# Inverse roots of the norms: a power on GpSimd in place of an integer guess and Newton steps on VectorE

## The chip, the cores and the metric

The kernel runs on one core of one Trainium2 chip. The metric is the device time of one execution in microseconds (us), as the median of several runs. Engine names are those of the profile: PE is TensorE (matmuls), PEld its weight loads, DVE is VectorE, ACT is ScalarE, POOL is GpSimd, SP is SyncE, which issues most of the DMAs.

## The reference

One inference step of a decoder layer with two groups of heads side by side: 2048 prompt rows of width 1024, and 8 single-row samples with states of their own. Cut to what matters here:

```python
EPS = 1e-6
def _rmsnorm(x, g):
    y = x * rsqrt(mean(x * x, axis=-1) + EPS)
    return y * g

hn = _rmsnorm(x, g_norm) * (1 + scale) + shift       # norm over 1024 columns
z = hn @ w_in                                        # one combined input projection
xa, za, q, k, v, glr, zg = split(z)
...                                                  # group 1: convolution, gates, linear recurrence
o, S_new = gla_chunked(q, k, v, log_alpha, S0)       # group 2: gated linear attention, 4 heads
o = o * rsqrt(mean(o * o, axis=-1) + EPS) * g_gla    # norm over a head's 256 columns
y_gla = o * silu(zg)
mix = concat([y_lru, y_gla]) @ w_out
x = x + gate * mix
return _rmsnorm(x, g_final), the new states
```

So there are three norms. The change touches the first (over x, 1024 columns) and the second (over each head's `o`, 256 columns). The final norm is computed by a function of its own, which is not changed.

## The kernel before

The 2048 rows are worked on in two halves of 1024. Rows lie on the 128 partitions wherever a norm is taken, so a sum of squares is one number per row and per tile, and an inverse root acts on a tile of 128 rows and one to four columns. The program has five stages in time: the start (the first half of x is loaded, normalized, transposed on PE and modulated, while PE computes the modulation from `w_ada`), half 0 (projections, then attention head by head in the order 3, 0, 1, 2, and the recurrence, in between the matmuls of the projections), half 1 (the same, with the samples), and from about 1119 us the output projection with residual and final norm, which is dense PE work.

`rsqrt` (L144) turns sums of squares `ss` into inverse roots `out`. It is called 37 times: five times at the start (`normalize` and `scales`, for pairs of 128-row tiles, `rs<-ss` 128x2, and once for the samples, 8x1), eight times in `turn_ahead` (L269: the second half of x, one tile of 128 rows at a time, while the first is worked on; `rs<-ss` 128x1), twenty times in `gla_norm` (L1138: for one head and one segment of rows, `ors<-oss`, 128x4 in half 0, 128x3 and 128x2 in half 1) and four times in `sample_out` (128x1). The sums of squares come from ACT (`junk` L173, an activation that accumulates).

Who waits for the result:
- At the start `times` (L187, its operation L189) multiplies x by it, and PE's transposes `tp<-ident,x` (L222) wait for that.
- In `turn_ahead` the products are transposed on DVE (L289) and stored; when the tile's buffer `xt` is free, SP loads the next one (L272), and ACT takes its squares (L173) in the midst of its other work.
- In `gla_norm` the attention output `on` is multiplied by it (L1143), and PE transposes `on` (L1217) after that.

Attention runs over segments of 512 rows in half 0, and of 384, 384 and 264 rows in half 1 (the last with the samples). `gla_start` (L1085) makes a segment's masked scores `am` (L1099), their rounded part `amh` (ACT) and the rest `aml` (L1102), and the transposed keys with rounded part `kTh` (ACT) and rest `kTl` (L1105). `gla_chunk` (L1111) then gives PE six or seven matmuls for 128 rows, in this order: `pkv` with `kTh` (L1121, L1122) and with `kTl` (L1123), then `po` with the state `S`, `amh` and `aml` (L1126 to L1129). DVE updates `S` (L1131, L1132) and copies `po` to `on` (L1135). The norm of a segment stands in time beside the `gla_start` of the next.

The order of instructions is set in three ways. Every engine runs its instructions strictly in order. The start is written in blocks marked `in_order`, which keep the written order on each engine. After it, work beside the projections is put on a clock (`after`, `tick`) and handed to a scheduler at build time, which orders the instructions of each engine by its own estimates of durations. So a change of one function may move instructions of others. POOL's queue also issues DMAs: weight loads and stores (`tr` L826, `twd` L838, `wd` L918, `r` L883), gate rows (`zs` L1265, `zgd` L1208), states. What stands behind a DMA issue that waits, waits too.

## Time and profile before

| | |
|---|---|
| median of 3 runs | 1440.75 us (1440.42 to 1440.96) |
| span of the profiled execution | 1444.3 us |
| PE busy | 1415.9 us, 98% |
| DVE busy | 1081.8 us, 75%, 2551 instructions |
| ACT busy | 678.9 us, 47% |
| POOL busy | 220.9 us, 15%, 362 instructions |
| PE's granted clock | 9 tenths or more in all 40 slices |

Of the profiled execution the page gives the span, and no separate time. All times of day below ("at 850 us") are from the start of that span. A row of the timeline reads: start, duration, engine, line, operation, output and inputs by the program's names, shape, count, and in brackets how long the engine sat idle before it and what it waited for last. A row may group several instructions of one kind, and the duration is then from the first's start to the last's end. The table of waits gives for each pair of waiting instruction and releaser the sum, the number of times and the longest.

### The profile page before, as it was taken

How to read it: one execution, taken by the hardware profiler on the slowest of the kernel's cores; microseconds unless marked ns; L12 is line 12 of the kernel's file. 1: busy time of each engine (PE TensorE's matmuls, PEld its weight loads, DVE VectorE, ACT ScalarE, POOL GpSimd, SP SyncE). 2: the span in 40 equal slices, each digit the busy share in tenths (PEclk: the TensorE clock that was granted, in tenths of full speed). 3: DMA queues.
4: the chain of work that ended last, by engine and by line, in shares of the span. 5: the costliest groups of instructions: out<-in, count | busy, mean ns of one | idle time of the engine just before them, and what ended most of it. 6: DMA issues, size and time to landing. Idle time of an engine off the chain costs nothing.

```text
span 1444.3 us, 23546 instructions
## 1 busy us (share of the span) xinstructions
PE 1415.9 (98%) x8677; PEld 1246.5 (86%) x8677; DVE 1081.8 (75%) x2551; ACT 678.9 (47%) x1227; POOL 220.9 (15%) x362
## 2 busy tenths in 40 slices
PE   7999999999999999999999999999999999999998
PEld 5889979888888988788899999999998887788886
DVE  5767658987798778935458688686888986688886
ACT  3653454653365255524354454635566622154342
POOL 0200112221112114000111422333210000000000
PEclk9999999999999999999999999999999999999999
DMA  9755785885676568567744665665671767694452
GB/s 328 271 186 176 248 260 200 267 283 191 215 234 209 190 199 281 183 234 239 287 144 150 206 237 177 226 197 182 239 251 67 292 231 271 226 351 144 136 168 113
DMA packets 176840, 313.75 MB, mean 217 GB/s; under 512 B 20370, under 2 KB 106034, under 8 KB 173901
## 3 DMA queue, kind: packets, MB, share of 16 engines
q1 hardware_dynamic: 122821, 225.82, 46.1%
q0 software_dynamic: 22912, 70.96, 14.2%
q10 hardware_dynamic: 30992, 15.47, 3.6%
q8 instruction: 68, 1.11, 0.3%
q14 instruction: 47, 0.39, 0.1%
HBM read 192.74 MB, written 119.53 MB: 216 GB/s over the span
## 4 chain that ended last, share of the span: by engine, by line
PE 75%; DVE 9%; issue 6%; ACT 4%; DMA 4%; POOL 1%; SPq 0%; DVEq 0%; POOLq 0%; ACTq 0%
PE acc L1898 12%; PE acc L714 10%; PE acc L716 10%; PE acc L715 9%; PE tp L1898 9%; PE acc L1612 6%; PE acc L399 3%; PE acc L400 3%; PE acc L401 3%; PE po L1126 1%; DMA tr<-in_w_in_dram 1%; DMA twd<-tr 1%; PE acc L1369 1%; PE tp L1095 1%; PE tp L1217 1%
## 5 line engine op out<-in xcount | busy, mean ns | idle before, releaser
L714 PE MATMUL acc<-hh,w 128*128 128x512 f32 (+3 forms) x1112 | 378.1, 340 | 2.2 <-DVE zs L1184 1.9
L715 PE MATMUL acc<-hl,w 128*128 128x512 f32 (+3 forms) x1112 | 375.8, 338 | 0.0
L716 PE MATMUL acc<-hh,w 128*128 128x512 f32 (+3 forms) x1112 | 375.6, 338 | 0.0
L714 PEld LDWEIGHTS acc<-hh,w 128*128 128x128 f32 x1112 | 209.8, 189 | 19.7 <-issue 3.0
L716 PEld LDWEIGHTS acc<-hh,w 128*128 128x128 f32 x1112 | 209.9, 189 | 16.4
L715 PEld LDWEIGHTS acc<-hl,w 128*128 128x128 f32 x1112 | 210.0, 189 | 15.4
L1898 PE MATMUL acc<-w,a 128*128 128x512 f32 (+1 forms) x792 | 184.8, 386 | 0.0
L1898 PEld LDWEIGHTS acc<-w,a 128*128 128x128 f32 x792 | 146.8, 188 | 33.2 <-issue 3.4
L399 PE MATMUL acc<-w,hh 128*128 128x256 f32 (+1 forms) x508 | 144.3, 284 | 0.6 <-DMA w<-parts 0.5
L400 PE MATMUL acc<-w,hh 128*128 128x256 f32 (+1 forms) x508 | 142.9, 281 | 0.0
L401 PE MATMUL acc<-w,hl 128*128 128x256 f32 (+1 forms) x508 | 142.9, 281 | 0.0
L1898 PE MATMUL tp<-w,a 128*128 128x512 f32 x564 | 136.0, 391 | 0.0
L1898 PEld LDWEIGHTS tp<-w,a 128*128 128x128 f32 x564 | 105.2, 188 | 26.8 <-issue 5.2
L399 PEld LDWEIGHTS acc<-w,hh 128*128 128x128 f32 x508 | 95.9, 189 | 2.1 <-DMA w<-parts 0.7
L401 PEld LDWEIGHTS acc<-w,hl 128*128 128x128 f32 x508 | 96.2, 189 | 0.0
L400 PEld LDWEIGHTS acc<-w,hh 128*128 128x128 f32 x508 | 95.8, 189 | 0.2
L1183 ACT ACTIVATE zs<-acc 128x512 f32<-128x512 f32 (+3 forms) x70 | 34.3, 490 | 103.3 <-PE acc L716 97.6
L1748 ACT CAST a<-s 128x512 fp32r<-128x512 f32 x61 | 36.5, 620 | 95.3 <-issue 35.8
L1332 DVE SCALAR_TENSOR_TENSOR cv<-xa,vecT,cv 128x512 f32<-128x512 f32 (+2 forms) x120 | 76.7, 642 | 3.5 <-ACT cv L1330 2.9
L1184 DVE SCALAR_TENSOR_TENSOR zs<-zs,acc 128x512 f32<-128x512 f32 (+3 forms) x70 | 38.4, 548 | 32.6 <-ACT zs L1183 32.5
L1010 ACT CAST vh<-acc 128x256 fp32r<-128x256 f32 x56 | 20.7, 369 | 83.3 <-PE acc L401 63.3
L1011 DVE TENSOR_TENSOR vl<-acc,vh 128x256 fp32r<-128x256 f32 x56 | 23.4, 420 | 44.2 <-ACT vh L1010 44.0
(402 smaller groups left out, 2761.6 us busy)
## 6 DMA issues: line engine op xcount, KB each, us to landing
parts<-w SPq DMA_DIRECT2D x37, 1024.0 KB
w<-parts SPq DMA_DIRECT2D x28, 1024.0 KB
wr<-in_w_in_dram SPq DMA_DIRECT2D x38, 512.0 KB
a<-mixd SPq DMA_DIRECT2D x63, 256.0 KB
w<-wd SPq DMA_DIRECT2D x12, 1024.0 KB
w<-twd SPq DMA_DIRECT2D x20, 512.0 KB
wada<-in_w_ada_dram SPq DMA_DIRECT2D x16, 512.0 KB
mixd<-zs ACTq DMA_DIRECT2D x32, 256.0 KB
```

The lines of the kernel that those rows point to most:

```text
L399: PE.matmul(ps, hh[:, kt, c], hi[:, kt % 4], start=kt == 0, stop=False)
L400: PE.matmul(ps, hh[:, kt, c], lo[:, kt % 4], start=False, stop=False)
L401: PE.matmul(ps, hl[:, kt, c], hi[:, kt % 4], start=False, stop=kt == KT - 1)
L714: PE.matmul(ps[:, :n], hi[:, kt], a, start=kt == 0, stop=False)
L715: PE.matmul(ps[:, :n], hi[:, kt], b, start=False, stop=False)
L716: PE.matmul(ps[:, :n], lo[:, kt], a, start=False, stop=kt == KT - 1)
L1183: S.activation(z, ps, AF.Tanh, scale=0.5)
L1184: V.scalar_tensor_tensor(z, z, 1.0, ps, op0=OP.add, op1=OP.mult)
L1332: V.scalar_tensor_tensor(cv[:, cq], xa[:, cq.start + k:cq.stop + k], cw[k], cv[:, cq], op0=OP.mult, op1=OP.add)
L1612: PE.matmul(ps, w[:, u, k], x[v][k], start=start and (k, u, v) == (0, 0, 0), stop=(k, u) == (3, 1), skip_group_check=True)
L1748: S.copy(t[:, 0, k], (low(t) if src is None else src)[:, k])
L1898: PE.matmul(ps, t[:, u, k], w[:, v, k, c], start=(q < 3 or ps is own) and (k, u, v) == (0, 0, 0), stop=(k, u) == (3, 1), skip_group_check= ...
```

## The change

`rsqrt` had twelve operations on DVE: mean plus EPS, a shift and a subtraction from a constant on the bits (a first guess), and three Newton steps of three operations each. Now it has two on POOL: mean plus EPS, and that to the power of -0.5. The exponent is a tile of 128x32 which POOL fills once at the start; it takes the place of a padding tile of the same size, and the two scratch tiles that are no longer used are still allocated, so every other tile keeps its address.

```diff
-    xp.tile([P, PAD_XP], F32, name="pad", bufs=1)
+    power = xp.tile([P, PAD_XP], F32, name="power", bufs=1)
+    G.memset(power, -0.5)
...
-    def rsqrt(pool, out, ss, n, rows, scale, q=V):
-
-        y = pool.tile([P, 16], F32, tag="rs_y", name="rs_y", bufs=1)[:rows, :n]
-        t = pool.tile([P, 16], F32, tag="rs_t", name="rs_t", bufs=1)[:rows, :n]
-        x = pool.tile([P, 16], F32, tag="rs_x", name="rs_x", bufs=1)[:rows, :n]
-        V.tensor_scalar(x, ss, scale, EPS, op0=OP.mult, op1=OP.add)
-        V.tensor_scalar(t.bitcast(I32), x.bitcast(I32), 1, None, op0=OP.logical_shift_right)
-        V.tensor_scalar(y.bitcast(I32), t.bitcast(I32), -1, 0x5F3759DF, op0=OP.mult, op1=OP.add)
-        for it in range(3):
...
-            V.tensor_tensor(t, y, y, op=OP.mult)
-            V.scalar_tensor_tensor(t, t, -0.5, x, op0=OP.mult, op1=OP.mult)
-            V.scalar_tensor_tensor(out if it == 2 else y, t, 1.5, y, op0=OP.add, op1=OP.mult)
+    def rsqrt(pool, out, ss, n, rows, scale):
+
+        x = [pool.tile([P, 16], F32, tag=f"rs_{k}", name=f"rs_{k}", bufs=1) for k in "ytx"][2][:rows, :n]
+        G.tensor_scalar(x, ss, scale, EPS, op0=OP.mult, op1=OP.add)
+        G.tensor_tensor(out, x, power[:rows, :n], op=OP.pow)
```

Line numbers after the change are smaller by 12 behind `rsqrt` (L1143 becomes L1131, and so on). The order of instructions moves in three places that the prediction speaks of.

The first is the start of POOL's queue. Before, it holds after the constants:

```order
L505 MEMSET rows 46x1024
L235 TENSOR_SCALAR hh<-hnf 128x2x256
L235 TENSOR_SCALAR hh<-hnf 128x512 x6
L235 TENSOR_SCALAR hh<-hnf 128x2x256 x8
L826 DMA tr<-in_w_in_dram 128x8x128 x2
```

And now (`hh<-hnf` is the rounding of the modulated x, `rs` the inverse roots of a pair of tiles):

```order
L493 MEMSET rows 46x1024
L148 TENSOR_SCALAR rs_x<-ss 128x2
L149 TENSOR_TENSOR rs<-rs_x,power 128x2
L148 TENSOR_SCALAR rs_x<-ss 128x2
L149 TENSOR_TENSOR rs<-rs_x,power 128x2
L223 TENSOR_SCALAR hh<-hnf 128x2x256
L223 TENSOR_SCALAR hh<-hnf 128x512 x6
L148 TENSOR_SCALAR rs_x<-ss 128x2
L149 TENSOR_TENSOR rs<-rs_x,power 128x2
```

The first two calls stand ahead of all rounding, the third among it.

The second place is DVE in half 0 at about 222 us of the trace, where head 0's first segment is normed while its second starts. Before:

```order
L1099 COPY_PREDICATED am<-mask,tp 128x512
L149 TENSOR_SCALAR rs_x<-oss 128x4
L1105 TENSOR_TENSOR kTl<-tp,kTh 128x512
L150 TENSOR_SCALAR rs_t<-rs_x 128x4
```

Here the remaining ten operations of the chain follow with others between them, and `on` after the last. Now:

```order
L1087 COPY_PREDICATED am<-mask,tp 128x512
L1093 TENSOR_TENSOR kTl<-tp,kTh 128x512
L1131 TENSOR_SCALAR on<-on,ors 128x256 x4
L1090 TENSOR_TENSOR aml<-am,amh 128x512
```

The products of `on` have moved ahead of `aml`.

The third place is DVE in half 1 at about 849 us, where the same happens with segments of 384 rows (`xt<-xt,smp` are products for the samples). Before:

```order
L1099 COPY_PREDICATED am<-mask,tp 128x384
L1109 TENSOR_SCALAR S_116<-S_116,f 128x256
L149 TENSOR_SCALAR rs_x<-oss 128x3
L1160 SCALAR_TENSOR_TENSOR xt<-xt,smp 128x256
L150 TENSOR_SCALAR rs_t<-rs_x 128x3
L1105 TENSOR_TENSOR kTl<-tp,kTh 128x384
L151 TENSOR_SCALAR rs_y<-rs_t 128x3
L1102 TENSOR_TENSOR aml<-am,amh 128x384
```

Now:

```order
L1087 COPY_PREDICATED am<-mask,tp 128x384
L1097 TENSOR_SCALAR S_117<-S_117,f 128x256
L1148 SCALAR_TENSOR_TENSOR xt<-xt,smp 128x256
L1131 TENSOR_SCALAR on<-on,ors 128x256 x3
L1090 TENSOR_TENSOR aml<-am,amh 128x384
L1093 TENSOR_TENSOR kTl<-tp,kTh 128x384
```

Here the products of `on`, which need the new inverse roots, stand ahead of both `aml` and `kTl`; before, they stood behind the whole chain, 22 rows further on. The same order comes again for the next two heads, at about 938 and 1028 us.

## The prediction

> **What bounds the kernel now.** I read the page's first part, then PE's waits, then the operations that go, then the places where PE waits for them.

> ```profile
> span 1444.3 us, 23546 instructions
> PE 1415.9 (98%) x8677; PEld 1246.5 (86%) x8677; DVE 1081.8 (75%) x2551; ACT 678.9 (47%) x1227; POOL 220.9 (15%) x362
> ```

> PE is busy for 98% of the span, and the change touches no matmul. So DVE's saving counts only where PE waits for DVE. The table of PE's waits names them (sum, times, longest):

> ```profile
> PE tp L1095 <- DVE xb L1080: 3.7, 3, 2.5
> PE tp L222 <- DVE x L189: 2.4, 4, 1.7
> PE po L1126 <- DVE on L1135: 1.4, 2, 1.0
> PE tp L1217 <- DVE on L1143: 0.8, 2, 0.5
> PE pkv L1123 <- DVE kTl L1105: 0.8, 3, 0.3
> PE tp L1219 <- DVE os L1179: 0.6, 2, 0.4
> ```

> All six together are 9.7 us, 0.7% of the span. This is the ceiling for what PE can gain at these waits, and the kTl row can as well grow. The output stage (from 1119 us) calls `rsqrt` nowhere.

> **The operations, removed and added.** The groups of DVE by line, and of POOL, busy and mean ns of one:

> ```profile
> L160 DVE SCALAR_TENSOR_TENSOR rs_t<-rs_t,rs_x 128x1 f32<-128x1 f32 (+4 forms) x111 | 17.7, 159 | 2.7
> L235 POOL TENSOR_SCALAR hh<-hnf 128x512 fp32r<-128x512 f32 x15 | 11.5, 772 | 58.5 <-ACT hnf L231 58.4
> L2297 POOL MEMSET const-float32-0.0<- 128x1 f32 x1 | 0.1, 98 | 0.2 <-issue 0.2
> ```

> 37 calls of 12 operations are 444; at about 160 ns that is 71 us of DVE's busy time removed (1081.8 to about 1011), nearly all beside PE's work. POOL gains 74 small operations and one memset at the start, before anything waits for it. How long a power takes no row shows. Below it is bounded by the memset of one column, 98 ns, above by twice the rounding of 512 columns, 1.5 us. The tiles have 1 to 4 columns, so it is nearer the first: I take 0.3 us for the power, 0.2 for mean plus EPS, 0.15 for the hops to POOL and on to DVE (0.10 and 0.03, below). So a call takes c = 0.65 us from the squares to the roots, with 0.35 and 1.85 as the ends.

> **The start.** DVE and PE where the second pair of tiles is normalized, and the hops at the first rounding:

> ```profile
> 20.77 0.17 DVE L149 TENSOR_SCALAR rs_x<-ss 128x2 f32<-128x2 f32 x1 [0.23 <-ACT junk L173]
> ...
> 23.15 1.42 DVE L189 TENSOR_SCALAR x<-x,rs 128x1024 f32<-128x1024 f32 x2
> ...
> 21.30 1.08 PE L546 MATMUL pa<-wada,sc 128*32 128x128 f32 x32
> 24.05 0.30 PE L222 MATMUL tp<-ident,x 128*128 128x128 f32 x1 [1.67 <-DVE x L189]
> 25.26 1.02 ACT L231 ACTIVATE hnf<-tp,Sh,Gm 128x256 f32<-128x256 f32 x2 [0.64 <-PE tp L222]
> 26.38 0.61 POOL L235 TENSOR_SCALAR hh<-hnf 128x512 fp32r<-128x512 f32 x1 [24.42 <-ACT hnf L231]
> 27.02 0.69 DVE L238 TENSOR_TENSOR hl<-hnf,hh 128x512 fp32r<-128x512 f32 x1 [0.28 <-POOL hh L235]
> ```

> The last three rows give the hops: ACT ends `hnf` at 26.28 and POOL starts at 26.38; POOL ends at 26.99 and DVE starts at 27.02. The twelve operations take 20.77 to 23.15, 2.38 us, with nothing between them, and PE stands still for 1.67 us behind them. With c the product starts 2.38 - 0.65 = 1.7 us earlier, and POOL is idle there, so this wait goes. The other three waits of the L222 row hold 0.7 us, behind the same chain and two more; most of them goes too. The ceiling is 2.4. What is late next is `w_ada`, which PE waits for at the first call already, and which streams at full rate at the second:

> ```profile
> 10.66 1.07 PE L546 MATMUL pa<-wada,sc 128*32 128x128 f32 x30 [1.05 <-DMA wada<-in_w_ada_dram]
> ...
> DMA  9999999999999999999999999999999999999954
> ```

> The second row is the DMA share of 20 to 45 us in 40 slices: full but for the last two. So what PE wins it may lose again before a later `pa<-wada`. I take -2.0, between -1.0 and -2.4. The first call I cost at nothing: `w_ada` holds PE until 10.66, and the transposes stand behind those matmuls.

> **Half 0.** Norms of the heads, and the load that a late chain delays:

> ```profile
> 226.41 1.14 DVE L1143 TENSOR_SCALAR on<-on,ors 128x256 f32<-128x256 f32 x4
> ...
> 226.90 1.14 PE L1217 MATMUL tp<-ident,on 128*128 128x128 f32 x8 [0.50 <-DVE on L1143]
> 255.60 0.44 PE L1217 MATMUL tp<-ident,on 128*128 128x128 f32 x2 [0.33 <-DVE on L1143]
> 252.24 0.90 POOL L826 DMA_DIRECT2D tr<-in_w_in_dram  x1 [4.90 <-issue]
> 294.45 0.15 DVE L149 TENSOR_SCALAR rs_x<-ss 128x1 f32<-128x1 f32 x1
> 296.56 0.16 DVE L161 SCALAR_TENSOR_TENSOR rs<-rs_t,rs_y 128x1 f32<-128x1 f32 x1
> 311.56 1.06 ACT L173 ACTIVATE junk<-xt 128x1024 bf16<-128x1024 f32 x1 [5.87 <-DMA xt<-in_x_prompt_dram]
> 295.56 1.06 ACT L1380 ACTIVATE tg<-tg 128x1024 f32<-128x1024 f32 x1
> 297.24 1.22 DVE L1385 SCALAR_TENSOR_TENSOR tg<-xl,tg 128x1024 f32<-128x1024 f32 x1
> ```

> At the first place `on` now follows `kTl`, ahead of work that came between, and its roots are there by then. Both of PE's waits for `on` go: -0.8. At the second place (255 us) POOL's queue holds the `tr` load ahead of the call. Its issue ended at 253.1, so the roots would come at 253.8, still ahead of PE's 255.60. But DVE, which reaches the products earlier now, would stand there for up to 3 us with other work behind it. The chain that it no longer runs (1.9 us of own time) covers the larger part; +1.5 is the upper end, -0.8 what I take.

> The 2.5 us wait for `xb` (322 us) goes back to ACT, which waited 5.87 us for `xt`. That load was issued when DVE had transposed the tile before, behind a chain that holds DVE from 294.45 to 296.7, 2.2 us. But only 0.6 us of this reaches the transposes: the product L1385 at 297.24 needs ACT's exponential, which ends at 296.62. In the new order a subtraction of 0.6 us (L836) leaves its place behind that product to one of 0.3 (`vl`). So -0.9, between 0 and -2.2. The seven other chains of `turn_ahead` delay nothing that PE waits for, and are costed at nothing: PE's own matmuls cover them, and without that cover each would cost or bring up to its 2.2 us.

> **Half 1: the loss.** Here the new order puts the products of `on` ahead of `kTl`:

> ```profile
> 849.37 0.19 ACT L173 ACTIVATION_READ_ACCUMULATOR junk<-on 128x1 f32 x1
> 849.67 0.47 DVE L1160 SCALAR_TENSOR_TENSOR xt<-xt,smp 128x256 f32<-128x256 f32 x1
> 850.13 0.55 DVE L1105 TENSOR_TENSOR kTl<-tp,kTh 128x384 fp32r<-128x384 f32 x1
> 850.74 0.38 PE L1123 MATMUL pkv<-vh,kTl 128*128 128x256 f32 x1 [0.26 <-DVE kTl L1105]
> 943.48 0.91 DVE L1143 TENSOR_SCALAR on<-on,ors 128x256 f32<-128x256 f32 x3
> 947.19 0.48 PE L1126 MATMUL po<-S,xb 128*128 128x256 f32 x1 [1.01 <-DVE on L1135]
> ```

> PE already waits for `kTl` here, so there is no slack at all. The squares end at 849.56; the roots come at 849.56 + c; then three products (0.91, some 0.08 of it beside what follows, an estimate), `aml` as long as `kTl` less the same overlap (0.47), and `kTl` 0.55: it ends at 851.41 + c. Before, it ended at 850.68 and PE started at 850.74. PE is late by 0.73 + c, about 1.4 us, and the `po` matmuls behind it in its queue wait with it. Three heads have this order: +4.2. In the other nine segments PE uses `kTl` late enough, or its own order moved along.

> Against it: the 1.01 us wait at 947.19 stands behind a DVE that is filled by a chain; with PE 1.4 us later and DVE one chain shorter it goes, -1.0. The samples' `os` (0.6 in the table) come earlier, -0.6. Half 1: +2.6.

> **The sum.** -2.0 - 0.8 - 0.9 + 2.6 = -1.1 us. The profiled 1444.3 becomes 1443.2. The profiled execution is 3.5 us (0.25%) longer than the median of the runs, and I carry the difference over: 1440.75 - 1.1 = 1439.6. What a measurement of this kernel can tell from no change is about 0.2%, 2.9 us.

> [...] When DVE works beside it, POOL's rounding takes longer:

> ```profile
> L214 POOL TENSOR_SCALAR hh<-fs x9: 612/1047/1050, 564.8 to 574.3; 128x512 fp32r<-128x512 f32 x9
> ```

> 612 ns alone, 1047 in the middle of DVE's two-input subtractions. [...]

> **Rivals.**
> - *Slower: the power is slow.* Each us on c costs three at the three heads and one at 21 us. The sum is -1.1 + 4 (c - 0.65), and passes +2.9 at c = 1.65, a power of 1.3 us. At the upper end, c = 1.85, it is +3.7: 1444.5. For it: no row of a power, and the spans of POOL are rough. Against: at four columns even a slow operation has little to do. [...]
> - *Faster: no stall at `kTl`.* If DVE reaches the `on` products later than I think, or the squares come earlier, so that only the reordering (0.73 each) costs, and the load at 306 us moves the full 2.2: -2.2 - 0.8 - 2.2 + 2.2 - 1.6 = -4.6, 1436.1. For it: DVE is 71 us lighter in all.
> - *POOL's queue blocks.* The call at 250 us behind the weight load: +1.5 in place of -0.3, sum +0.7: 1441.5.

> **How the numbers follow.** My sum, with its small unknowns (1438 to 1441.5): 0.42. The queue that blocks, with waits of POOL behind DVE's operations: 0.08. The slow power: 0.23. The fast case: 0.27. Faster by over 0.2% is the fast case and a little of mine, 0.32. Slower is most of the slow power and a little of the queue, 0.22. Within is the rest, 0.46. The range, 1435 to 1444.3, runs from a little beyond the fast case's 1436.1 to just short of the slow case's end, and leaves out 2 in 10 beyond both.

> **What would show it.** Right: about 2100 DVE instructions; PE's wait at 24 us gone; `pkv` L1111 waiting for `kTl` three times for over 1 us in half 1; `tp` L1205 waiting for `on` no more. Wrong: power operations over 1 us; DVE idle before `on` for more than 1 us, released by POOL; a POOL issue ahead of a root; the wait for `xb` at 322 us unchanged or gone.

## The result and the profile after

The changed kernel takes 1456.51 us (median of 4 runs, 1453.28 to 1458.1) against 1440.86 us for the kernel before, a ratio of 1.0094 (95% interval 1.0078 to 1.0109): slower by about 14 us (11 to 16 by the interval). The forecast was 1439.6, between 1435.0 and 1444.3; it was wrong in size and in sign. The profiled execution took 1455.96 us.

The page's first lines, and PE's waits, of the changed kernel (line numbers are 12 smaller than before):

```profile
span 1454.2 us, 23214 instructions
PE 1415.3 (97%) x8677; PEld 1245.1 (86%) x8677; DVE 1024.8 (70%) x2107; ACT 677.8 (47%) x1227; POOL 264.4 (18%) x437
```

```profile
PE pkv L1111 <- DVE kTl L1093: 10.6, 7, 2.4
PE pa L534 <- DMA wada<-in_w_ada_dram: 3.4, 4, 1.1
PE tp L1083 <- DVE xb L1068: 2.8, 3, 1.6
...
PE acc L1357 <- ACT xh L1344: 1.5, 1, 1.5
...
PE acc L1358 <- DVE xl L1345: 0.7, 1, 0.7
PE tp L210 <- DVE x L177: 0.7, 2, 0.4
PE tp L210 <- ACT hnf L219: 0.7, 1, 0.7
```

DVE lost 57 us of busy time and 444 instructions. (Their durations add up to 71.9 us, as the forecast had it; but rows of DVE overlap at their ends, as `aml` and `kTl` below by 0.08 us, so its busy time fell by less.) What PE lost stands in the first row: the wait for `kTl`, 0.8 us before, is 10.6 us now. The wait for `x` at the start fell from 2.4 to 0.7, and the row of `on` (0.8) is gone.

The new operations, by shape (busy, mean ns of one):

```profile
L149 POOL TENSOR_TENSOR ors<-rs_x,power 128x4 f32<-128x4 f32 x8 | 8.3, 1036 | 0.7
L149 POOL TENSOR_TENSOR ors<-rs_x,power 128x3 f32<-128x3 f32 x8 | 7.0, 880 | 0.7
L149 POOL TENSOR_TENSOR ors<-rs_x,power 128x2 f32<-128x2 f32 x4 | 2.9, 714 | 0.3
L149 POOL TENSOR_TENSOR ors<-rs_x,power 128x1 f32<-128x1 f32 x4 | 2.3, 572 | 0.3
L148 POOL TENSOR_SCALAR rs_x<-oss 128x2 f32<-128x2 f32 x4 | 0.8, 191 | 0.3
```

A power for the heads and samples took about 0.42 us and 0.155 us more for each of its 1 to 4 columns, where I had taken 0.3 us. The eight one-column powers for x took 0.71 us on average instead of 0.57. The first power of all, at 8.75 us, took 0.72 us, and the second of its shape, at 19.96 us, 0.70. The place at which the forecast saw the loss, head 0 at 850 us, shows the whole chain:

```profile
849.07 0.19 ACT L161 ACTIVATION_READ_ACCUMULATOR junk<-on 128x1 f32 x1
849.18 0.48 DVE L1148 SCALAR_TENSOR_TENSOR xt<-xt,smp 128x256 f32<-128x256 f32 x1
849.43 0.28 POOL L148 TENSOR_SCALAR rs_x<-oss 128x3 f32<-128x3 f32 x1 [5.88 <-ACT junk L161]
849.80 0.88 POOL L149 TENSOR_TENSOR ors<-rs_x,power 128x3 f32<-128x3 f32 x1
850.72 0.88 DVE L1131 TENSOR_SCALAR on<-on,ors 128x256 f32<-128x256 f32 x3 [1.05 <-POOL ors L149]
851.51 0.55 DVE L1090 TENSOR_TENSOR aml<-am,amh 128x384 fp32r<-128x384 f32 x1
851.98 0.55 DVE L1093 TENSOR_TENSOR kTl<-tp,kTh 128x384 fp32r<-128x384 f32 x1
852.59 0.58 PE L1111 MATMUL pkv<-vh,kTl 128*128 128x256 f32 x1 [2.41 <-DVE kTl L1093]
```

The squares end at 849.26 and the products start at 850.72: c is 1.46 us instead of 0.65. It consists of 0.17 for the hop to POOL, 0.28 for mean plus EPS, 0.09 between the two, 0.88 for the power and 0.04 for the hop back. DVE stands idle for 1.05 us of it, then makes `on`, `aml` and `kTl` in that order, and PE waits 2.41 us where it had waited 0.26.

What came behind that wait was not in the forecast. The view by windows (PE busy, PEld, DVE, ACT and POOL busy, then PE's granted clock, DMA share, GB/s):

```profile
849.00:852.60 3.60, 1.19 (x9) 0.79 (x7) 2.54 (x9) 1.03 (x4) 1.17 (x2) 0.95 0.46 110
852.60:855.00 2.40, 2.40 (x8) 2.22 (x9) 2.07 (x10) 0.00 (x0) 0.84 (x1) 0.50 0.70 288
855.00:857.00 2.00, 2.00 (x11) 2.00 (x11) 1.90 (x10) 0.00 (x0) 0.00 (x0) 0.84 0.75 262
857.00:860.00 3.00, 3.00 (x22) 2.96 (x21) 0.27 (x1) 0.60 (x2) 1.52 (x2) 1.00 0.44 175
```

After the wait PE is granted half its clock until 855.6, and then all of it again. The trace's clock records show three such drops in the body of this execution (278.8, 852.2, 1036.6 us), each 3.41 us long at 0.50, so 1.7 us of PE's work each. The profile before had four (12, 26, 326 and 592 us). Its execution was a long one: in every run whose time and span are both known the time is 1.7 to 2.3 us more than the span, so its 1444.3 us of span stand some 5 us above its median, and not 3.5, as the forecast had it by comparing a span with a time. A second profile of the kernel before (below) has a span of 1440.2 us and no drop after the start. Against it, the start times of PE's n-th matmul show where the 14 us of span come from (PE's order is nearly the same in both; worked out from the two traces):

| PE's matmul | time in the first profile before | changed minus second profile before, us |
|---|---|---|
| 600th, in the start | 74 | -2.8 |
| 1900th | 275 | -4.7 |
| 2100th | 305 | -0.3 |
| 2300th | 347 | +1.7 |
| 4300th, before half 1's attention | 725 | +2.1 |
| 5300th | 850 | +3.8 |
| 5500th | 881 | +8.3 |
| 6500th | 1001 | +10.0 |
| 7300th, output stage | 1132 | +14.2 |

So there was a gain in the first 275 us, and then three losses: 4.4 us at 275 to 305, 1.9 us at 305 to 347, and 12 us in half 1. The second of them can't be put down to the change: in the same stretch the first profile before loses 3.4 us against the second, with the same program.

### The profile page after: what moved, and what is told of

It reads as the page before. It is cut to its first block, busy times and chain, and to the rows that moved or that the text cites. A ratio compares the mean times of both kernels' runs of the same rounds, so it can differ in the third digit from the quotient of the medians.

```text
span 1454.2 us, 23214 instructions
## 1 busy us (share of the span) xinstructions
PE 1415.3 (97%) x8677; PEld 1245.1 (86%) x8677; DVE 1024.8 (70%) x2107; ACT 677.8 (47%) x1227; POOL 264.4 (18%) x437
## 4 chain that ended last, share of the span: by engine, by line
PE 73%; DVE 9%; DMA 5%; ACT 5%; issue 4%; POOL 2%; SPq 0%; DVEq 0%; ACTq 0%; POOLq 0%
PE acc L1886 12%; PE acc L702 9%; PE acc L704 9%; PE acc L703 9%; PE tp L1886 9%; PE acc L1600 6%; PE acc L387 3%; PE acc L388 3%; PE acc L389 3%; PE po L1114 2%; DVE cv L1320 1%; DMA w<-parts 1%; DMA wada<-in_w_ada_dram 1%; DMA xt<-in_x_prompt_dram 1%; DVE tg L1376 1%
```

## The experiments

The comparisons are with runs of the kernel before on the same chip; their medians were 1442.5 (25 runs), 1442.6 (19) and 1442.7 (17).

**Which calls cost: `start_on_pool` and `heads_on_pool`.** A function `newton` with the old twelve operations is added, and either the calls for heads and samples or those for x use it:

```diff
 start_on_pool:
-        rsqrt(gp, rs[:, :nch], ss[:, :nch], nch, P, 1.0 / DV)
+        newton(gp, rs[:, :nch], ss[:, :nch], nch, P, 1.0 / DV)
-        rsqrt(gp, rs[:, :1], ss[:, :1], 1, P, 1.0 / DV)
+        newton(gp, rs[:, :1], ss[:, :1], 1, P, 1.0 / DV)
 heads_on_pool:
-        rsqrt(pool, rs[:m, :n], ss[:m, :n], n, m, 1.0 / D)
+        newton(pool, rs[:m, :n], ss[:m, :n], n, m, 1.0 / D)
```

> The thirteen calls for x (start and turn_ahead) use the power on GpSimd, the twenty-four for the heads and samples the twelve VectorE operations as before. Theory (the loss comes from the heads' calls in half 1, where the products of on stand ahead of kTl): PE's waits for kTl fall from 10.6 us to about 0.8 as before, and the time is 1438 to 1440, 1 to 2 us below before's 1440.9. Rival (GpSimd's queue around 250 us and its weight loads carry a good part of the loss): 1443 or more, with PE's losses around 275 us still there.

> The reverse: only the calls for the heads and samples use the power, those for x the VectorE chain. Theory: the loss of half 1 is all here: 1456 to 1459, at or up to 2 us above the changed kernel's 1456.5, since the gain at the start is missing; PE's waits for kTl about 10.6 us. Rival (the queue behind the calls for x makes up part of it): 1448 to 1453.

`start_on_pool` took 1443.22 us, ratio 1.0006 (0.9993 to 1.0018): no difference from before, above the 1438 to 1440 of the theory. The time is the rival's, but not its mechanism: the trace has no wait for `xh` or `xl` around 275 us, and 0.8 us for `kTl` as before. `heads_on_pool` took 1457.69 us, 1.0104 (1.0084 to 1.0123), as the theory had it: the whole loss belongs to the heads' and samples' calls. Its waits for `kTl` are those of the changed kernel:

```profile
PE pkv L1123 <- DVE kTl L1105: 10.6, 7, 2.4
```

**The price of the power: `mult` and `two_powers`.** The same program, once with a product in place of the power (the roots are not computed), once with every power computed twice:

```diff
 mult:
-        G.tensor_tensor(out, x, power[:rows, :n], op=OP.pow)
+        G.tensor_tensor(out, x, power[:rows, :n], op=OP.mult)
 two_powers:
         G.tensor_tensor(out, x, power[:rows, :n], op=OP.pow)
+        G.tensor_tensor(out, x, power[:rows, :n], op=OP.pow)
```

> The changed kernel with a product in place of the power (same operands and the same order on every engine; the inverse roots are not computed, so outputs differ). Theory A (the power's own 0.85 us is on the path at the seven kTl waits): each call gets shorter by 0.5 to 0.65 us, PE's kTl waits fall from 10.6 to 6 to 7.5 us, the waits at about 850, 943 and 1034 us from 2.4 to about 1.8, and the time to 1450 to 1453. Rival B (only the order matters): kTl waits stay above 9 us and the time above 1454.

> The changed kernel with every power computed twice in a row into the same tile (order of the engines unchanged). Theory A (the call's length is on PE's path at kTl): each call longer by 0.55 us (1 column) to 1.03 us (4 columns), PE's waits for kTl grow by 0.9 us at three or two columns each time, from 10.6 us to 16 to 18, the longest from 2.4 to about 3.3, and the time to 1463 to 1468 (the six waits, some 3 us more around 250 to 280 us, and a clock drop after nearly every long wait). Rival B (only the order matters): 1456 to 1459.

`mult` took 1447.99 us, 1.0037 (1.0022 to 1.0052), `two_powers` 1470.51 us, 1.0195 (1.0167 to 1.0222). The product's duration (minimum, median, maximum, in ns) and PE's waits of both, `mult` first:

```profile
L149 POOL TENSOR_TENSOR ors<-rs_x,power x24: 191/198/288, 111.1 to 1064.8; 128x4 f32<-128x4 f32 x8, 128x3 f32<-128x3 f32 x8, 128x2 f32<-128x2 f32 x4, 128x1 f32<-128x1 f32 x4
PE pkv L1111 <- DVE kTl L1093: 5.8, 6, 1.7
```

```profile
PE pkv L1112 <- DVE kTl L1094: 17.8, 8, 3.4
```

The longest wait is 1.7, 2.4 and 3.4 us with calls that are 0.68 us apart and then 0.97: PE waits out the call's length to the tenth of a microsecond. The times move by more than the waits, by 8.5 us and 14 us for 4.8 and 7.2 us of waiting. Some of the rest are other places of half 0 and the samples, and some are drops of the clock behind the start: two in the profile of `mult`, three in the changed kernel's and six in that of `two_powers`. Both medians came out beyond the range that I had given, on the side of a larger effect; for `two_powers` it is that of two runs, 1467.43 and 1473.58, the lower of which is inside.

**The order: `behind_keys`.** The products of `on` are queued behind `kTl` of the next segment; the power stays on GpSimd:

```diff
 def chunks(s, c):
                 prep[s, "run"] = gla_start(half, h, s, prep[s])
+                if s:
+                    with behind(V):
+                        prep[s, "product"]()
...
-            gla_norm(nch, prep[s, "run"])
+            prep[s + 1, "product"] = gla_norm(nch, prep[s, "run"], s + 1 < ns)
```

> The changed kernel with the products of on queued behind kTl of the next segment; GpSimd's and ScalarE's order is the same, the power too. Theory A (the place of the products ahead of kTl is the cause): PE's kTl waits fall from 10.6 us to 1 to 2 and the clock no longer drops there, so 1443 to 1446. Rival B (the power's latency costs wherever it stands, since on is needed soon after): the waits move to on (L1131) before the transposes, and the time stays above 1450.

It took 1442.70 us, 1.0003 (0.9992 to 1.0014), just below the expected 1443 to 1446. The loss is gone, and the power is still on GpSimd; the order of GpSimd, ScalarE and SyncE is the changed kernel's. What moved is the place of the products on DVE, with the few operations around them (45 in all), and behind it three groups of PE's matmuls at about 870, 962 and 1055 us, where `kTl` and `po` of a last segment stand earlier. At the other four places of a long wait for `kTl` PE's order is the changed kernel's too. The same place as above, DVE and then PE:

```profile
845.64 0.56 DVE L1093 TENSOR_TENSOR kTl<-tp,kTh 128x384 fp32r<-128x384 f32 x1
846.12 0.55 DVE L1090 TENSOR_TENSOR aml<-am,amh 128x384 fp32r<-128x384 f32 x1
846.70 0.88 DVE L1133 TENSOR_SCALAR on<-on,ors 128x256 f32<-128x256 f32 x3
```

```profile
846.25 0.38 PE L1111 MATMUL pkv<-vh,kTl 128*128 128x256 f32 x1
```

`kTl` and `aml` take the 1.05 us that DVE spent waiting, the roots are there when DVE comes to `on` (no bracket on that row), and PE doesn't wait for `kTl` anywhere: the table of its waits has no such row. Rival B falls.

**The queue: `half0_on_pool` and `one_call`.** In the changed kernel the call at 248 us, which the forecast had named as a rival, stands behind the weight load. Two waits of PE follow 28 us later, which the kernel before doesn't have:

```profile
246.98 0.90 POOL L814 DMA_DIRECT2D tr<-in_w_in_dram  x1 [6.33 <-ACT tx L1360]
248.23 1.03 POOL L149 TENSOR_TENSOR ors<-rs_x,power 128x4 f32<-128x4 f32 x1
249.30 1.15 DVE L1131 TENSOR_SCALAR on<-on,ors 128x256 f32<-128x256 f32 x4 [2.17 <-POOL ors L149]
277.54 0.50 PE L1357 MATMUL acc<-xh,wg 128*128 128x512 f32 x1 [1.52 <-ACT xh L1344]
278.77 0.80 PE L1358 MATMUL acc<-xl,wg 128*128 128x512 f32 x1 [0.73 <-DVE xl L1345]
```

`half0_on_pool` puts only the eight calls of half 0's heads on GpSimd; `one_call` is the changed kernel with this one call back on VectorE:

```diff
 half0_on_pool (and the calls for x and samples by newton):
-        rsqrt(gp, rs[:, :nch], ss[:, :nch], nch, P, 1.0 / DV)
+        (newton if half else rsqrt)(gp, rs[:, :nch], ss[:, :nch], nch, P, 1.0 / DV)
 one_call:
+        (newton if (half, h, s) == (0, HEADS[1], 1) else rsqrt)(gp, rs[:, :nch], ss[:, :nch], nch, P, 1.0 / DV)
```

> Only the eight calls for the heads in half 0 on GpSimd, all others as before. Theory A: half 0 alone costs its 2.7 us around 275 us less 0.8 for the two waits for on, 1443 to 1446; PE's kTl waits 0.8 us as before. Rival B (half 0 is neutral, the loss there came from the calls for x in the same queue): 1441 to 1443.

> The changed kernel, but the one call of half 0 whose two GpSimd operations stand behind a weight load in GpSimd's queue (second segment of the second head, at 248 us) is made by the twelve VectorE operations. Theory A (the queue is the cause of the waits for xh and xl at 275 to 279 us): DVE's wait of 2.17 us ahead of on goes, PE's 2.7 us of losses there go, and the time is 2 to 4 us below the changed kernel's (1452 to 1454). Rival B (the other order of ScalarE's casts, which wait for stores of twd, is the cause): PE's losses at 275 us stay above 2 us and the time at 1455 to 1457.

`half0_on_pool` took 1445.79 us, 1.0023 (1.0013 to 1.0034): half 0 by itself costs some 3 us, as theory A had it. `one_call` took 1454.74 us (1453.06 to 1456.59), about 1.8 us below the changed kernel (the two were not run side by side, and the intervals of their ratios, 1.0066 to 1.0097 and 1.0078 to 1.0109, overlap). The expected 2 to 4 us were not reached. But PE's waits between 270 and 285 us are gone altogether in its trace, and the wait for `xh` is no longer in its table. So that one call caused these waits. How much of it is the queue and how much the power, `mult` tells, where ScalarE's order around 250 us is the changed kernel's (so that rival B can't make the difference):

```profile
247.25 0.91 POOL L814 DMA_DIRECT2D tr<-in_w_in_dram  x1 [5.86 <-ACT tx L1360]
248.50 0.20 POOL L149 TENSOR_TENSOR ors<-rs_x,power 128x4 f32<-128x4 f32 x1
248.74 1.14 DVE L1131 TENSOR_SCALAR on<-on,ors 128x256 f32<-128x256 f32 x4 [1.41 <-POOL ors L149]
```

With an operation of 0.20 us in the power's place DVE still stands for 1.41 of the 2.17 us, and PE's two waits are 0.7 us each instead of 1.5 and 0.7. So the larger part is the load ahead of the call, the smaller the power.

**Versions meant to be better: `combined` and `behind_one`, and second profiles.** `combined` has the calls for x on GpSimd, half 0's heads and the samples by `newton`, and half 1's heads on GpSimd behind `kTl`. `behind_one` is `behind_keys` with the one call of `one_call` on VectorE. `before_again` and `behind_again` are second profiles of the kernel before and of `behind_keys`.

```diff
 combined, against behind_keys:
-                if s:
+                if half and s:
-        rsqrt(gp, rs[:, :nch], ss[:, :nch], nch, P, 1.0 / DV)
+        (rsqrt if half else newton)(gp, rs[:, :nch], ss[:, :nch], nch, P, 1.0 / DV)
 behind_one, against behind_keys:
-        rsqrt(gp, rs[:, :nch], ss[:, :nch], nch, P, 1.0 / DV)
+        (newton if one else rsqrt)(gp, rs[:, :nch], ss[:, :nch], nch, P, 1.0 / DV)
```

> A version meant to keep the gains: the calls for x on GpSimd, those for the heads in half 0 and for the samples by the twelve VectorE operations, those for the heads in half 1 on GpSimd with the products queued behind kTl. Theory A (gains and losses are where the traces show them): 1.5 to 3 us below before in the same state of the clock, 1439 to 1441.5. Rival B (what is won at the start is given back to the loads of w_ada, and the rest is neutral): within 1 us of before, 1442 to 1443.5.

> The version with the products behind kTl, and the one call behind the weight load at 248 us made by VectorE again: both repairs together. Theory A (each repair removes its own loss): PE's 1.0 us at 275 us and its wait for vl go, 1440 to 1442, 0.5 to 2 us below before on the same chip. Rival B (what is left is set by waits that the change never touched, and by the scheduler's order around them): within 1 us of before, 1442 to 1444.

> The kernel before once more, for a second profile. Theory A (the clock halves for one window of 3.41 us when PE was idle for more than about 1.8 us of the window before, on a fixed grid): the drops lie at multiples of 3.413 us from each other, only behind the waits of 1.4 us and longer (8 to 11, 24, 325, 592, 1105 us), and never after a window with less than 1.4 us idle. Rival B (drops come at random): some elsewhere. The wait for x at 24 us is 1.67 us again, that for xb about 2.5.

> The version with the products behind kTl once more, for a second profile. Theory A (what the start wins is given back to the loads of w_ada, by an amount that varies from run to run): PE's waits up to 110 us sum to 5 to 7.5 us against before's 8.2, with w_ada alone between 0.9 and 3.4. Rival B (the gain at the start is fixed): 5.2 us again, w_ada 0.9.

`combined` took 1444.57 us, 1.0015 (1.0006 to 1.0024): slower than before, against both expectations. Two waits of its table are long:

```profile
PE tp L1095 <- DVE xb L1080: 3.7, 3, 2.5
...
PE tp L1224 <- DVE os L1184: 1.8, 2, 1.4
```

The first is no explanation, since it is the same in the first profile before and 4.0 us in `behind_one`, the fastest version. The second is 0.6 us before and at most 1.5 in the other versions. Another 0.4 us lies outside the span: all eleven runs of `combined` take 2.2 us more than their span, those of before 1.8. What makes the rest of the 2 us is open. Each mixture of calls gives the scheduler another problem, and it moves other work.

`behind_one` took 1440.89 us, 0.9986 (0.9975 to 0.9998): about 2 us below before, as its theory A had it. It is the only version whose interval lies below 1, and by so little that, among nine versions, it may be chance. In its trace the waits at 275 us are gone, but that for `vl` stays at 1.0 us, against the expectation. `before_again` took 1441.94 us with a span of 1440.2. Its drops lie at 11.6 (two in a row) and 25.2 us, 13.65 us apart, which is 4 x 3.413. The waits for `x` and `xb` are:

```profile
PE tp L222 <- DVE x L189: 2.4, 4, 1.7
...
PE tp L1095 <- DVE xb L1080: 1.9, 3, 1.0
```

The wait for `xb` was 3.7 us in all in the first profile, of which 2.53 at one place, 325 us. That place is now 0.76 us, and the longest, 0.96, is another one at 190 us, which both profiles have: the same program, another execution. Here the expectation of "about 2.5" was wrong. `behind_again` took 1443.56 us. The waits of PE up to 110 us for `w_ada`, in `behind_keys`, `behind_again` and `behind_one`:

```profile
PE pa L534 <- DMA wada<-in_w_ada_dram: 0.9, 2, 0.5
```

```profile
PE pa L534 <- DMA wada<-in_w_ada_dram: 2.2, 3, 1.1
```

```profile
PE pa L546 <- DMA wada<-in_w_ada_dram: 3.2, 5, 1.0
```

With 1.0 us before. All three have the wait for `x` at 0.7 or less, so they win 1.7 us or more at `x`, and give back between nothing and 2.2 us at `w_ada`, and 0.7 to 0.8 at `hnf`, a new wait. All waits of PE up to 110 us sum to 8.2 and 7.9 us in the two profiles before, to 5.2 in `behind_keys`, 6.4 in `behind_again` (its theory A had 5 to 7.5), 7.1 in `behind_one` and 7.8 in the changed kernel.

## Why the prediction was wrong

Four steps failed: the size of c, the sentence on the other nine segments, a clock that has no term in the sum, and the low price of POOL's queue. The gains that were to stand against the loss (the start above all) came out smaller, too.

- **The mechanism of half 1 was right, its size was not.** The place (the products of `on` ahead of `kTl`, three heads), the formula (PE late by 0.73 + c) and the slope hold: with the measured c of 1.46 the formula gives 2.19 us more, and the trace shows 2.41 - 0.26 = 2.15. The step that failed is the one that took c as 0.65, with a power of 0.3 us chosen as "nearer the first" of its two ends. The power of three columns takes 0.88, the first operation 0.28 instead of 0.2, and hops and gap 0.30 instead of 0.15. By my own sum with c = 1.46, -1.1 + 4 x 0.81 = +2.1. The rival "the power is slow" was the right one, and this far it would still have been inside the range.
- **"In the other nine segments PE uses `kTl` late enough, or its own order moved along" was wrong.** Seven waits instead of three: four more of 0.7 to 0.9 us, 3.4 us in all, at 764, 873, 965 and 1057 us. Two of them:

```profile
764.63 0.38 PE L1111 MATMUL pkv<-vh,kTl 128*128 128x256 f32 x1 [0.66 <-DVE kTl L1093]
873.40 0.39 PE L1111 MATMUL pkv<-vh,kTl 128*128 128x256 f32 x1 [0.91 <-DVE kTl L1093]
```

  At 764 us PE's order is as before, and DVE's is that of the three heads: it stands 1.05 us for the roots, then makes `on`, `aml` and `kTl`, and PE comes late enough to lose only 0.66 us. At the other three PE's order had moved back, but DVE's `kTl` had moved back more, behind `on` and other work, and DVE had waited 1.0 to 1.1 us for the roots.
- **No term for the clock.** A wait of PE was counted at its length. Of the nine waits of 2.4 us in the changed kernel, `heads_on_pool` and `one_call`, six were followed by 3.41 us or more at half clock, 1.7 us more each. Two of the three waits at 850, 943 and 1034 us had that in the profile, and the one at 278 us. The mean granted clock of the changed kernel's four runs, 0.994, against 0.997 for 61 runs of before, is 3 to 4 us of PE time at 1440 us.
- **The queue at 250 us** was among the rivals, at a price of +1.5 for half 0 and a chance of 0.08. It happened: 2.17 us of DVE and 2.2 us of waits at PE. What I had wrong was that PE would feel it at `on`; it feels it at the convolution (`xh`, `xl`), which stood behind `on` in DVE's queue.
- **Half 0's gains.** The waits for `on` (0.8) went, as predicted. The 0.9 us from the load at 306 us had no firm ground: the wait that it was to shorten is 2.5 us in one execution of the kernel before and 0.8 in another, and 1.6 in the changed kernel.
- **The start** has the forecast's number, but hardly by the forecast's way. The 600th matmul comes 2.8 us earlier, against -2.0 forecast. But PE's waits up to 110 us are 7.8 us in all, against 8.2 and 7.9 before. The 1.7 us won at `x` went back to `w_ada` (3.4 us instead of 1.0) and `hnf`, so the gain of 0.1 to 0.4 us falls short of the forecast's smallest, 1.0. The forecast's list of six waits also left out this one of the kernel before, at 9 us, which the trace puts down to the first call's chain:

```profile
PE pa L546 <- DVE rs_t L150: 1.4, 1, 1.4
```

  It is gone in the changed kernel, but there `w_ada` holds PE for 0.8 us at the same matmul. What makes the 600th matmul earlier is mostly the clock: the second profile before has three windows at half speed there, the changed kernel none. The drop at 25 us, which comes behind the wait of 1.67 us for `x`, is in three of the four profiles with Newton steps for x and in none of the nine with these calls on GpSimd. So removing that wait seems to have a worth that the forecast had no term for. In time it can't be told from nothing (`start_on_pool`, ratio 1.0006).
- **The two gains of half 1** came out in part. The wait of 1.0 us at 947 us went. The samples' `os`, 0.6 us, was to go and is 0.8 us.
- **The range** was bounded by c = 1.85 alone, through three places. The measured c lies inside its ends; the missing places, the clock, the queue and the gains that did not come are what put the time 12 us above the top. As an estimate from the rows above: -1.1 forecast, +5.6 for `kTl` (9.8 us more instead of 4.2), +2.2 for `xh` and `xl`, +1.6 to 1.9 for the waits of the start, +0.9 for `xb`, +0.8 for `os` and 3 to 4 for the clock make 13 to 14 us, against the measured 13.6 (0.94%). Several of these terms vary by a microsecond between executions, so that the agreement is partly luck.

Among the forecast's chances are waits of POOL behind DVE's operations. At the three heads the trace has them at 0.1 us each. At 849.43 mean plus EPS took 0.28 us instead of 0.19, and ended at 849.71, 0.05 us after DVE's product of `xt` (849.18 to 849.66), which had begun before the squares ended (849.26); at the other two heads it took 0.28 and 0.29 us and ended 0.05 and 0.06 us after that product. Beside a longer operation of DVE it took longer:

```profile
795.70 1.20 POOL L148 TENSOR_SCALAR rs_x<-oss 128x1 f32<-128x1 f32 x1
795.64 1.22 DVE L1372 SCALAR_TENSOR_TENSOR tx<-tx,cv 128x1032 f32<-128x1032 f32 x1
```

An operation of 0.19 us took 1.20 here, and ended 0.05 us after DVE's. The forecast's rounding of 612 ns "alone" is not alone: it began at 568.65, ahead of DVE's `hl` at 568.72, which then took 1.08 us instead of 0.69.

## What to carry to other kernels

A chain moved to another engine is priced by its latency, hop and operation, wherever the new order makes the first engine wait for it. Look at what stands behind that wait in its queue; here the repair was another order, not another operation. Freed time on an engine that is not the bound was worth next to nothing here: 57 us off VectorE gave no gain that the time shows (`behind_keys`), and three waits of 2.4 us with four shorter ones, which came with it, cost some 12 us. Price an operation that the trace doesn't show by its upper bound when it decides, and take a second profile before a wait for a DMA becomes a term of a sum.

## What the runs showed of the hardware

**A small power on GpSimd** took 0.57, 0.71, 0.88 and 1.04 us for 1 to 4 columns of 128 rows (means for the heads and samples), a product of the same shapes 0.20 us (median).

**Mean plus EPS on GpSimd took longer in 15 of its 37 calls, and 13 of these ended just after an operation of VectorE.** In the changed kernel it took 0.18 to 0.20 us in 22 calls and 0.23 to 1.20 us in the other 15; 13 of these ended 0.05 to 0.06 us after an operation of VectorE, of one or two inputs, that had begun earlier. Beside others, such as `am` at 869 us or `kTl` at 220 us, it took 0.19 us.
